# RWKV-7 / RG-LRU / cross-attention step: TensorE's order in the chunk chain fixed, and 48 projection steps ahead of the inverse instead of 37

## The chip, the cores and the metric

The kernel runs on one core of one Trainium2 chip. The metric is the device time of one launch in microseconds (us), the median of several runs. TensorE (PE in the profile, with its weight loads as PEld) multiplies; VectorE (DVE), ScalarE (ACT) and GpSimd (POOL) do the elementwise work; SyncE (SP) issues most DMAs. Each engine takes its instructions in a fixed order, and waits on semaphores for the others.

## The reference, cut to what matters

One layer for 512 prompt tokens and 8 samples of 8 tokens (N = 576 columns), width 1024. One projection feeds three branches; each is gated and projected, the three are merged, and an output projection and a norm follow:

```python
u, za, xb, zb, q, zc, gates = split_in(rmsnorm(x, g_norm) @ w_in)
oa, s_last, shift_last = rwkv7_branch(u, za, ...)   # 16 heads of 64
ob, h_last, conv_last = rglru_branch(xb, zb, ...)
oc = cross_attn(q, zc, mem_k, mem_v)
merged = g_a * (oa @ w_br_a) + g_b * (ob @ w_br_b) + g_c * (oc @ w_br_c)
y = rmsnorm(x + merged @ w_out, g_final)
```

The RWKV-7 branch is a recurrence over time with a 64x64 state per head:

```python
sa = einsum("bhvk,bhk->bhv", s, -kk_t)
s  = s * w_t + sa * (kk_t * a_t) + v_t * k_t      # outer products
o_t = einsum("bhvk,bhk->bhv", s, r_t)
```

## The kernel before, in words

**Projections as fill.** Each product of a 128-row block of weights with the 576 activations is a `Unit`. Weights and activations are each split into a high and a low part (`whi` by ACT at L280, `wlo` by DVE at L281; `xh`, `xl`), and three of the four products are summed. `Stream.step` issues one step: one of 8 slices of the inner dimension, 3 products on 2 halves of the columns, so 6 matmuls of 128x288 (L355). A unit is 8 steps. `st.go(n)` puts n steps into the program. Units come from two lists: `first` (what is needed next: the `u` units of the RWKV input, the `za` units of its gate) and, when that is empty, `fill` (`spill_units`, in this order: 24 gate units `g`, 8 `zc`, 8 `xb`, 8 `zb`), whose results are spilled to memory. A `zc` unit costs, besides its matmuls, one ACT pass and two DVE passes (L411, L415), a load of `ocd` and a store to `ocz`; a `g` unit has one ACT pass and a store.

**The RWKV branch** (`rwkv_phase`) takes the 16 heads as 8 pairs in 4 groups of 2 pairs, and time in 8 prompt chunks of 64 tokens; a ninth "chunk" holds the 64 sample tokens. For each group: prepare (`prep_a`, `prep_b`, `prep_c`); the products `m` (L990); `invert`, which sends 32x32 triangular blocks through memory to DVE, inverts them there in 60 small operations (`Xt`, `X`, L1016 and L1018), copies (`XT`, L1022) and sends them back (`M`, `xz`); meanwhile on PE `direct` (`R`, `Zt`), `bonus` (`bon`, L959 and L960) and `st.go(37)`. Then `invert2` joins the 32-blocks to 64-blocks (`z` L1041, `w` L1050, with ACT copies between), `solved` makes `U` and `W`, and `chain` goes through the 8 chunks: `A` = `ZR` times the state (L1128, whole 128x128 matmuls), DVE adds it to `UV` (`plus_state`, L1121), `go(2)`, the new state's part `dS` (L1137), the output `A<-UV,M` (`outs`, L1113), `go(4)`. The sample state goes along: `sample_a` (load `sn`, transposes `s0t`) in chunks 1 and 4, `sample_b` (`A8`, L1189) in 2 and 5, `sample_c` (`dSs`, L1202, transposes `s1t`, store) in 3 and 6.

**Two kinds of matmul.** Projections, `A` from the state and transposes use the whole array (128*128 in the profile's rows). `z`, `w`, `U`, `W`, `dS`, `outs`, `A8` and `dSs` give a `tile_position` and use 32 or 64 of its columns (32*32, 128*64, 128*32); they are called tiled here, and a tiled run is a stretch of PE's program that holds only such matmuls.

**The order.** A scheduler, which works from its own estimate of readiness, orders each engine's instructions when the kernel is built; what stands in the program is a proposal. So the steps of later units, of the next chunk's `go` and of the sample work end up between the matmuls of a chunk.

**After the groups:** `gn_a`, `gn_t`, `gn_b` normalise the output and multiply by the gate `za`, and store it (`oad`). Then the rest of the `zb` units; `load_split` loads the attention output (`oxl<-ocz`, on SP), splits it into `oh` (ACT, L592) and `ol` (DVE, L593) for the 8 branch units `br` of branch c; then those of branch a beside the RG-LRU (`lru_phase`), of branch b, and the output projection (`final`, `fo`).

Of the kernel before, what the change touches and what calls it, by code (L numbers as in the profile page):

```python
# [46 lines left out]
class Kern:  # L47
    def __init__(self, ctx, tc, ins, outs):
# [7 lines left out]
        self.dq = 0  # L56

# [4 lines left out]
    def transpose(self, out, in_, rows):  # L62

        self.nc.tensor.transpose(out, in_, self.ident[:rows, :rows])  # L64
# [240 lines left out]
class Stream:  # L305
# [24 lines left out]
    def step(self):  # L330
# [22 lines left out]
        for q, (a, b) in enumerate(((hi, xh), (hi, xl), (lo, xh))):  # L353
            for o, t0, m in parts:
                nc.tensor.matmul(self.ps[:, o:o + m], a[:, k, :], b[:, k, t0:t0 + m],  # L355
                                 start=(k == 0 and q == 0), stop=(k == KC - 1 and q == 2))
# [111 lines left out]
def lru_phase(K, o2, then):  # L468
# [4 lines left out]
    with tc.tile_pool(name="lruc", bufs=1, reuse_waits="tile") as lc, tc.tile_pool(name="lru", bufs=2, reuse_waits="tile") as lp:  # L473
# [31 lines left out]
        def gates(j):  # L505
# [5 lines left out]
            for q, bh in enumerate((K.bah, K.bxh)):  # L511
                g = lp.tile([P, N], F32, tag=f"g{q}", name=f"g{q}")
                for s in range(2):
                    pg = K.psb(f"pg{q}")[:, 0:HN]
                    cs = slice(HN * s, HN * s + HN)
                    nc.tensor.matmul(pg, wbd[q][:, j, :], xc[:, cs], start=True, stop=True)
# [143 lines left out]
def attention(K, xp, qs, qf, kv):  # L660
# [6 lines left out]
    def p_scores(h, n):  # L667
# [45 lines left out]
    def s_keys(g, b):  # L713
# [88 lines left out]
def rwkv_phase(K):  # L802
# [5 lines left out]
    with ExitStack() as es:  # L808
# [90 lines left out]
        def prep_a(o):  # L899
# [5 lines left out]
            for s in range(2):  # L905
                cs = slice(HN * s, HN * s + HN)
                for n, (dst, bias) in enumerate(((tw, K.w0h), (ta, K.a0h))):
                    pl = K.psb("lora")[:, 0:HN]
                    nc.tensor.matmul(pl, wlh[:, n, :], xw2[n][:, cs], start=True, stop=False)
                    nc.tensor.matmul(pl, wll[:, n, :], xw2[n][:, cs], start=False, stop=True)  # L910
# [15 lines left out]
        def prep_b(o):  # L926
# [25 lines left out]
        def bonus(o):  # L952
# [3 lines left out]
            for s in range(2):  # L956
                cs = slice(HN * s, HN * s + HN)
                pb = K.psb("bon")[:, 0:HN]
                nc.tensor.matmul(pb, K.bones, hi[:, cs], start=True, stop=False)  # L959
                nc.tensor.matmul(pb, K.bones, lo[:, cs], start=False, stop=True)  # L960
                nc.vector.tensor_mul(o.bon[:, cs], pb, o.v[:, cs])

        def prep_c(o):
# [71 lines left out]
        def invert2(prs):  # L1035
            for g0 in (0, 9):
                pzs = [K.psb("z1") for o in prs]
                for g in range(g0, g0 + 9):
                    for o, pz in zip(prs, pzs):
                        a, b = o.br, o.br + 32  # L1040
                        nc.tensor.matmul(pz[b:b + 32, 32 * (g - g0):32 * (g - g0) + 32], o.M1[a:a + 32, g, b:b + 32],  # L1041
# [5 lines left out]
                for g in range(g0, g0 + 9):  # L1047
                    for o, pw in zip(prs, pws):
                        a, b = o.br, o.br + 32
                        nc.tensor.matmul(pw[a:a + 32, 32 * (g - g0):32 * (g - g0) + 32], o.xz[b:b + 32, g, :],  # L1050
# [5 lines left out]
        def direct(prs):  # L1056

            r0 = prs[0].r0 = [rt.tile([P, N], F32, tag="k", name="r0") for _ in range(2)]
            for c0, n in ((0, 4), (4, 4), (8, 1)):
                pR = K.psb("R")  # L1060
                for c in range(c0, c0 + n):
                    for h in range(2):
                        for o in prs:
                            a, b, m = o.kr, o.br, P * (c - c0) + C * h
                            nc.tensor.matmul(pR[b:b + 64, m:m + C], o.M1[a:a + 64, 2 * c + h, b:b + 64],
# [7 lines left out]
            for c0 in (1, 5):  # L1073
                pZ = K.psb("Zt")
                for c in range(c0, c0 + 4):
                    for o in prs:
                        b, m = o.br, P * (c - c0)
                        nc.tensor.matmul(pZ[b:b + 64, m:m + P], o.ZR[:, c, 1 - o.q, :], K.ident, start=True, stop=True,
# [3 lines left out]
        def solved(prs):  # L1082

            r0, zt = prs[0].r0, prs[0].zt
            for c0, n in ((0, 4), (4, 4), (8, 1)):
                pU = K.psb("U")
                for c in range(c0, c0 + n):
                    for h in range(2):
                        for o in prs:
                            b, m = o.br, P * (c - c0) + C * h  # L1090
                            rhs = r0[c // 4][b:b + 64, m:m + C] if c < 8 else r0[h][b:b + 64, P * 4:N]
                            nc.tensor.matmul(pU[b:b + 64, m:m + C], o.M1[b:b + 64, 2 * c + h, b:b + 64],
# [15 lines left out]
        def outs(os, c, pA, first):  # L1108

            for h in range(2):  # L1110
                for o in os:
                    a, m = o.kr, P * o.q + C * h
                    nc.tensor.matmul(pA[a:a + 64, m:m + C], o.M1[:, 2 * c + h, a:a + 64], o.UV[:, c, C * h:C * h + C],  # L1113
                                     start=first, stop=(h == 1) or first, tile_position=(0, a), skip_group_check=True)
# [8 lines left out]
        def chain(os, c):  # L1123
            cur, nxt = sbd[(c + 1) % 2], sbd[c % 2]
            pA = K.psb("A")
            if c > 0:
                for o in os:
                    nc.tensor.matmul(pA[:, P * o.q:P * o.q + P], o.ZR[:, c].rearrange("p a b -> p (a b)"), cur[:, o.q, :],  # L1128
                                     start=o is os[0], stop=False, skip_group_check=True)
# [378 lines left out]
```

## Time and profile before

| what | value |
|---|---|
| median of 3 runs | 1184.54 us (1183.98 to 1185.02) |
| the profiled execution's own time | 1184.47 us |
| its span on the core | 1182.7 us |
| mean granted TensorE clock | 0.992 |
| PE / DVE / ACT / POOL busy | 1145.4 / 713.2 / 517.3 / 184.3 us |

The span is what the profile's instructions cover; 1.8 us of the execution lie around it. A group of rows counts matmuls as the chip runs them: an fp32 one is two of the program's where it uses the tiled form (`dS` x4 is `dS` x2 in the program). Busy time of pipelined matmuls overlaps, so a matmul's cost is read from the start of one to the start of the next.

### The profile page before, as it was taken

The page shows a single profiled execution, that of the slowest core. Times are in us where ns is not written, and L with a number is a line of the kernel's source. Part 1 is how long each engine was busy: PE and PEld are TensorE (multiplying, and loading weights), DVE is VectorE, ACT ScalarE, POOL GpSimd, SP SyncE. Part 2 cuts the span into 40 slices and gives each one's busy share as a digit, 9 for nine tenths or more (in the row PEclk, how much of TensorE's full clock was granted, in tenths as well). Part 3 has the DMA queues.
Part 4 walks back from the last instruction along what each step waited for, and adds up shares of the span by engine and source line. Part 5 has one row for each costly group of instructions (what it writes and reads, how often), then busy time and mean ns, then how long its engine had stood idle before and what let it go on. Part 6 is the DMA issues. An engine that isn't in the chain of part 4 may idle for free.

```text
span 1182.7 us, 25731 instructions
## 1 busy us (share of the span) xinstructions
PE 1145.4 (97%) x10567; PEld 1068.8 (90%) x10567; DVE 713.2 (60%) x1436; ACT 517.3 (44%) x1004; POOL 184.3 (16%) x311
## 2 busy tenths in 40 slices
PE   6999999999999999999999999999999999979997
PEld 4998877899998898988989989999889999979997
DVE  5345655238764687835788457874455386975633
ACT  5444544337324374243752336532444266442333
POOL 3010001010003210022100130101211012570031
PEclk9999999999999999999999999999999999998999
DMA  4447685522452233532233522345337665348412
GB/s 140 130 145 233 211 254 189 162 81 66 107 140 73 65 93 82 142 89 70 78 92 120 145 73 65 106 125 149 85 90 232 203 195 170 104 115 261 117 45 81
DMA packets 220623, 151.50 MB, mean 128 GB/s; under 512 B 52640, under 2 KB 196106, under 8 KB 220506
## 3 DMA queue, kind: packets, MB, share of 16 engines
q1 hardware_dynamic: 217242, 146.87, 42.1%
q10 hardware_dynamic: 3264, 2.99, 0.9%
q8 instruction: 83, 1.36, 0.5%
q14 instruction: 34, 0.28, 0.1%
HBM read 120.82 MB, written 29.01 MB: 127 GB/s over the span
## 4 chain that ended last, share of the span: by engine, by line
PE 79%; DVE 7%; ACT 5%; issue 3%; DMA 3%; POOL 2%; SPq 0%; DVEq 0%; ACTq 0%; POOLq 0%
PE u L355 13%; PE g L355 12%; PE br L355 9%; PE xb L355 4%; PE zc L355 4%; PE za L355 4%; PE fo L1349 4%; PE q L355 4%; PE zb L355 3%; PE kv L355 2%; PE m L990 1%; PE dS L1137 1%; DVE wlo L281 1%; DMA wraw<-in_w_mem_kv 1%; PE skt L64 1%
## 5 line engine op out<-in xcount | busy, mean ns | idle before, releaser
L280 ACT CAST whi<-wraw 128x1024 fp32r<-128x1024 f32 x129 | 135.4, 1050 | 292.6 <-PE g L355 90.7
L281 DVE TENSOR_TENSOR wlo<-wraw,whi 128x1024 fp32r<-128x1024 f32 x128 | 158.9, 1241 | 127.5 <-ACT whi L280 126.7
L355 PE MATMUL u<-xh,whi 128*128 128x288 f32 x400 | 92.2, 305 | 0.0
L355 PE MATMUL br<-oh,wlo 128*128 128x288 f32 x384 | 84.4, 302 | 4.4 <-DVE wlo L281 4.3
L355 PE MATMUL u<-xl,whi 128*128 128x288 f32 x400 | 88.6, 300 | 0.0
L355 PE MATMUL u<-xh,wlo 128*128 128x288 f32 x400 | 88.6, 299 | 0.0
L355 PE MATMUL br<-oh,whi 128*128 128x288 f32 x384 | 85.4, 305 | 3.0 <-ACT oh L592 2.9
L355 PE MATMUL g<-xh,whi 128*128 128x288 f32 x384 | 86.6, 304 | 0.0
L355 PE MATMUL g<-xh,wlo 128*128 128x288 f32 x384 | 84.7, 300 | 0.0
L355 PE MATMUL g<-xl,whi 128*128 128x288 f32 x384 | 84.4, 301 | 0.0
L355 PE MATMUL br<-ol,whi 128*128 128x288 f32 x384 | 84.2, 301 | 0.0
L355 PEld LDWEIGHTS u<-xh,whi 128*128 128x128 f32 x400 | 65.1, 188 | 5.5 <-issue 4.1
L355 PEld LDWEIGHTS br<-oh,wlo 128*128 128x128 f32 x384 | 63.5, 194 | 5.6 <-DVE wlo L281 5.6
L355 PEld LDWEIGHTS br<-oh,whi 128*128 128x128 f32 x384 | 63.7, 193 | 4.3 <-ACT oh L592 3.4
L355 PEld LDWEIGHTS u<-xl,whi 128*128 128x128 f32 x400 | 64.7, 188 | 2.0 <-issue 1.4
L355 PEld LDWEIGHTS u<-xh,wlo 128*128 128x128 f32 x400 | 64.7, 188 | 0.9 <-issue 0.2
L355 PEld LDWEIGHTS g<-xh,whi 128*128 128x128 f32 x384 | 62.3, 190 | 3.2 <-issue 3.1
L355 PEld LDWEIGHTS g<-xh,wlo 128*128 128x128 f32 x384 | 62.7, 190 | 1.2 <-issue 1.2
L355 PEld LDWEIGHTS br<-ol,whi 128*128 128x128 f32 x384 | 63.4, 193 | 0.1
L355 PEld LDWEIGHTS g<-xl,whi 128*128 128x128 f32 x384 | 62.4, 190 | 1.1 <-issue 1.1
L1016 DVE TENSOR_TENSOR Xt<-X 72x30 f32<-72x30 f32 (+14 forms) x120 | 39.3, 328 | 11.4 <-DMA X<-d 7.8
L1349 PE MATMUL fo<-wol,oh 128*128 128x256 f32 (+1 forms) x160 | 45.0, 282 | 0.0
(386 smaller groups left out, 2894.3 us busy)
## 6 DMA issues: line engine op xcount, KB each, us to landing
wraw<-in_w_in SPq DMA_DIRECT2D x89, 512.0 KB
wraw<-in_w_mem_kv SPq DMA_DIRECT2D x16, 512.0 KB
kn<-in_cache_mem_k SPq DMA_DIRECT2D x16, 512.0 KB
kn<-in_cache_mem_v SPq DMA_DIRECT2D x16, 512.0 KB
gd<-flt SPq DMA_DIRECT2D x24, 288.0 KB
gtt<-gd SPq DMA_DIRECT2D x24, 288.0 KB
wraw<-in_w_br_c SPq DMA_DIRECT2D x8, 512.0 KB
wraw<-in_w_br_a SPq DMA_DIRECT2D x8, 512.0 KB
```

Source lines behind the costliest of these rows:

```text
L64: self.nc.tensor.transpose(out, in_, self.ident[:rows, :rows])
L280: nc.scalar.copy(hi, raw)
L281: eng.tensor_sub(lo, raw, hi.bitcast(F32))
L355: nc.tensor.matmul(self.ps[:, o:o + m], a[:, k, :], b[:, k, t0:t0 + m], start=(k == 0 and q == 0), stop=(k == KC - 1 and q == 2))
L990: nc.tensor.matmul(pms[h][64 * w:64 * w + 64, P * (c - c0):P * (c - c0) + P], BK[64 * h:64 * h + 64, c, w, :], ZR[64 * h:64 * h + 64, c].r ...
L1016: nc.vector.tensor_mul(tv, X[:, 0:s, s:s + 1].to_broadcast([NQ, s, m]), X[:, s:s + 1, s + 1:].to_broadcast([NQ, s, m]))
L1137: nc.tensor.matmul(pS[hs, C * o.q:C * o.q + C], o.BKn[:, c, hs], o.UV[:, c, hs], start=True, stop=True, tile_position=(0, 64 * h))
L1349: nc.tensor.matmul(pos[t][:r, :W], a[:, k, t * P:t * P + r], b[:, k, :], start=(k == 0 and q == 0), stop=(k == KC - 1 and q == 2))
```

## The change

It adds a flag `K.pin` and a helper `K.mm`; while the flag is set (over the chain of a group) every matmul and transpose keeps its place in the program. The chain is rewritten so that a chunk has one stretch of whole matmuls (`A`, `full()`, 12 of fill) and one of tiled ones (`dS`, `outs`, `tiled()`), and then 24 of fill. The sample work is cut into five pieces, which are handed to chosen chunks; the load of `sn` is a piece of its own, ahead of the chain for the first pair and in chunk 3 for the second. And 48 steps stand ahead of the inverse's use instead of 37. The number of matmuls is the same. The core of the diff:

```diff
     def transpose(self, out, in_, rows):
-        self.nc.tensor.transpose(out, in_, self.ident[:rows, :rows])
+        ins = self.nc.tensor.transpose(out, in_, self.ident[:rows, :rows])
+        if self.pin:
+            self.tc.keep_in_program_order(ins)
+
+    def mm(self, *a, **kw):
+        ins = self.nc.tensor.matmul(*a, **kw)
+        if self.pin:
+            self.tc.keep_in_program_order(ins)
...
-        def chain(os, c):
+        def chain(os, c, full, tiled):
...
                 plus_state(os, c, pA)
+            full()
+            if c > 0:
                 st.go(2)
...
             outs(os, c, pA, c == 0)
             for o in os:
                 o.cur = nxt[:, o.q, :]
+            tiled()
             st.go(4)
...
-            st.go(37)
+            st.go(48)
...
+            fulls = {1: lambda: sample_a(o0), 4: lambda: sample_c(o0), 5: lambda: sample_a(o1)}
+            tileds = {2: lambda: sample_b(o0), 3: lambda: [sample_o(o0), sample_in(o1)],
+                      6: lambda: sample_b(o1), 7: lambda: sample_o(o1)}
+            sample_in(o0)
+            K.pin = True
             for c in range(8):
-                chain(prs, c)
-                if c in (1, 4):
-                    sample_a(prs[c // 4])
-                if c in (2, 5):
-                    sample_b(prs[c // 4])
-                if c in (3, 6):
-                    sample_c(prs[c // 4])
+                chain(prs, c, fulls.get(c, none), tileds.get(c, none))
+            K.pin = False
+            sample_c(o1)
```

`sample_o` holds the sample rows' `outs` and `dSs`, cut from `sample_b` and `sample_c`. In the changed kernel's rows every matmul has line L71 and every transpose L65, and other lines are up to 20 further down.

What this does to the order is seen at three places. **First, PE in chunk 1 of the first group's chain** (`u`, `g`: fill; `s0t`: a sample transpose). Before:

```order
L355 MATMUL u_4386<-xl,whi 128x288 x2
L355 MATMUL u_4386<-xh,wlo 128x288 x2
L1137 MATMUL dS<-UV,BKn 64x64 x2
L64 MATMUL s0t<-ident,sn 128x128
L1137 MATMUL dS<-UV,BKn 64x64 x2
L1113 MATMUL A<-UV,M_3281 64x64
L1113 MATMUL A<-UV,M_3428 64x64
```

Now:

```order
L71 MATMUL g_4038<-xh,whi 128x288 x2
L71 MATMUL g_4038<-xl,whi 128x288 x2
L71 MATMUL g_4038<-xh,wlo 128x288 x2
L71 MATMUL dS<-UV,BKn 64x64 x4
L71 MATMUL A<-UV,M_3281 64x64
L71 MATMUL A<-UV,M_3428 64x64
```

Before, the four `dS` stand in two tiled runs with a transpose between; now in one, and the fill beside them is of `g` units where it was of `u` units. Over the whole program the tiled runs go from 144 to 92. In the four chains, `U` and `W` with chunk 0 left out, they go from 64 (17, 17, 15 and 15) to 28 (7 each); in `invert2`, `solved` and chunk 0 from 5 a group to 1.

**Second, DVE in the inverse of group 2** (`flt`: results of fill units; `zc_7900`: one such unit in PSUM). Before:

```order
L1018 TENSOR_TENSOR X<-X,Xt 72x9x22
L1016 TENSOR_TENSOR Xt<-X 72x210
L1018 TENSOR_TENSOR X<-X,Xt 72x10x21
L1016 TENSOR_TENSOR Xt<-X 72x220
L1018 TENSOR_TENSOR X<-X,Xt 72x11x20
```

Now:

```order
L1027 TENSOR_TENSOR X<-X,Xt 72x9x22
L290 TENSOR_TENSOR wlo<-wraw,whi 128x1024
L1025 TENSOR_TENSOR Xt<-X 72x210
L420 SCALAR_TENSOR_TENSOR flt<-flt,zc_7900 128x576
L1027 TENSOR_TENSOR X<-X,Xt 72x10x21
L424 SCALAR_TENSOR_TENSOR flt<-flt 128x576
L1025 TENSOR_TENSOR Xt<-X 72x220
```

The 60 operations of the inverse are the same. Between the first of them and `XT` stand 4 `wlo`, 1 `wls` and 4 `flt` operations before, and 5, 1 and 10 now; in groups 0 and 1 the count is unchanged, and in group 3 there are 4 `wlo` and no `flt` operation now, where there were 4 and 4.

**Third, PE and SP behind the last chain.** PE before, at the end of the last `za` unit:

```order
L355 MATMUL za_10853<-xl,whi 128x288 x2
L355 MATMUL za_10853<-xh,wlo 128x288 x2
L64 MATMUL ro<-ident,shst 125x128
L64 MATMUL ro<-ident,shst 100x128
L355 MATMUL zb_10971<-xh,whi 128x288 x2
L355 MATMUL zb_10971<-xl,whi 128x288 x2
```

PE now:

```order
L71 MATMUL za_11207<-xl,whi 128x288 x2
L71 MATMUL za_11207<-xh,wlo 128x288 x2
L65 MATMUL ro<-ident,shst 125x128
L65 MATMUL ro<-ident,shst 100x128
L71 MATMUL br_11354<-oh,whi 128x288 x2
L71 MATMUL br_11412<-oh,whi 128x288
L71 MATMUL br_11354<-ol,whi 128x288 x2
```

SP now, from the first pair's `oad` on:

```order
L61 DMA oad<-oT 128x576
L61 DMA out_shift_p<-rowbuf 25x128
L61 DMA out_shift_s<-rowbuf 100x128 x2
L61 DMA wraw<-in_w_br_c 128x8x128
L61 DMA oad<-oT 128x576
L61 DMA oxl<-ocz 128x576 x8
```

Between the last `za` matmul and the first `br` matmul PE had six `zb` units (288 matmuls); now it has two transposes, since the fill lists have run out. On SP the eight `oxl` loads stand behind the second `oad`, as they did before (there in two parts, of 5 and 3).

More of the change, by code (lines that the diff above doesn't have):

```diff
@@ L515, in gates @@
                     cs = slice(HN * s, HN * s + HN)
-                    nc.tensor.matmul(pg, wbd[q][:, j, :], xc[:, cs], start=True, stop=True)
+                    K.mm(pg, wbd[q][:, j, :], xc[:, cs], start=True, stop=True)
                     nc.scalar.activation(g[:, cs], pg, AF.Tanh, bias=bh[:, j:j + 1], scale=0.5)
@@ L931, in prep_b @@
             for c in range(NCH):
-                nc.tensor.matmul(pr_[br:br + 64, 2 * c:2 * c + 2], o.sq[:, C * c:C * c + C], K.bones2, start=True, stop=True,
+                K.mm(pr_[br:br + 64, 2 * c:2 * c + 2], o.sq[:, C * c:C * c + C], K.bones2, start=True, stop=True,
                                  tile_position=(0, br))
@@ L958, in bonus @@
                 pb = K.psb("bon")[:, 0:HN]
-                nc.tensor.matmul(pb, K.bones, hi[:, cs], start=True, stop=False)
-                nc.tensor.matmul(pb, K.bones, lo[:, cs], start=False, stop=True)
+                K.mm(pb, K.bones, hi[:, cs], start=True, stop=False)
+                K.mm(pb, K.bones, lo[:, cs], start=False, stop=True)
                 nc.vector.tensor_mul(o.bon[:, cs], pb, o.v[:, cs])
@@ L1077, in direct @@
                         b, m = o.br, P * (c - c0)
-                        nc.tensor.matmul(pZ[b:b + 64, m:m + P], o.ZR[:, c, 1 - o.q, :], K.ident, start=True, stop=True,
+                        K.mm(pZ[b:b + 64, m:m + P], o.ZR[:, c, 1 - o.q, :], K.ident, start=True, stop=True,
                                          tile_position=(0, b))
@@ L1112, in outs @@
                     a, m = o.kr, P * o.q + C * h
-                    nc.tensor.matmul(pA[a:a + 64, m:m + C], o.M1[:, 2 * c + h, a:a + 64], o.UV[:, c, C * h:C * h + C],
-                                     start=first, stop=(h == 1) or first, tile_position=(0, a), skip_group_check=True)
+                    K.mm(pA[a:a + 64, m:m + C], o.M1[:, 2 * c + h, a:a + 64], o.UV[:, c, C * h:C * h + C],
+                         start=first, stop=(h == 1) or first, tile_position=(0, a), skip_group_check=True)
             for o in os:
@@ L1136, in chain @@
                     hs = slice(C * h, C * h + C)
-                    nc.tensor.matmul(pS[hs, C * o.q:C * o.q + C], o.BKn[:, c, hs], o.UV[:, c, hs], start=True, stop=True,
-                                     tile_position=(0, 64 * h))
+                    K.mm(pS[hs, C * o.q:C * o.q + C], o.BKn[:, c, hs], o.UV[:, c, hs], start=True, stop=True,
+                         tile_position=(0, 64 * h))
             pS3 = pS[:, 0:G * C].rearrange("p (q v) -> p q v", v=C)
@@ L1168, in sample_a @@
                     nc.sync.dma_start(sn[64 * b2:64 * b2 + 64, :, 64 * h:64 * h + 64], src[b2])
+        def sample_a(o):
+            sn = o.sn
             pt = K.psb("s0t")
@@ L1201, in sample_c @@
                 hs = slice(C * h, C * h + C)
-                nc.tensor.matmul(pS[hs].rearrange("p (b v) -> p b v", v=C), o.BKn[:, 8, hs], o.uvx[:, :, hs],
-                                 start=True, stop=True, tile_position=(0, 64 * h))
+                K.mm(pS[hs].rearrange("p (b v) -> p b v", v=C), o.BKn[:, 8, hs], o.uvx[:, :, hs],
+                     start=True, stop=True, tile_position=(0, 64 * h))
             nc.vector.tensor_add(s1, s1, pS.rearrange("p (b v) -> p b v", v=C))
+        def sample_c(o):
+            s1 = o.s1
             so = big("so")[:, 0:4, :]
```

49 lines of the change are left out of this document (26 added, 23 removed).

## Prediction

> **What bounds the kernel now.** I read the page first, then the windows of the stages that the change touches, then timelines of single places. From the page:
>
> ```profile
> span 1182.7 us, 25731 instructions
> PE 1145.4 (97%) x10567; PEld 1068.8 (90%) x10567; DVE 713.2 (60%) x1436; ACT 517.3 (44%) x1004; POOL 184.3 (16%) x311
> PE   6999999999999999999999999999999999979997
> PEclk9999999999999999999999999999999999998999
> ```
>
> PE is busy nearly everywhere; the one slice below 9 between the ends is the 37th. So time can be won only by making PE's own work denser, and is lost wherever PE has to wait. The windows of the inverse in group 2, of the `zb` units behind the last chain, and of the RG-LRU's end (PE busy, PEld, DVE, ACT, POOL, granted clock, DMA share, GB/s):
>
> ```profile
> 621.00:663.00 42.00, 42.00 (x329) 41.80 (x328) 33.95 (x81) 10.77 (x16) 3.80 (x4) 1.00 0.47 135
> 897.00:936.00 39.00, 39.00 (x295) 39.00 (x295) 18.17 (x21) 15.54 (x23) 0.06 (x2) 1.00 0.74 242
> 1035.00:1065.00 30.00, 22.99 (x151) 21.48 (x151) 24.05 (x25) 12.46 (x18) 23.51 (x24) 0.93 0.41 115
> ```
>
> In the first two PE has no idle time: the fill covers a wait of other engines. In the third it idles 7.0 of 30 us. The amount of fill is fixed, so the change can only move this cover: 11 steps in each of 4 groups. A step is 6 matmuls; `zb` below takes 38.40 us for 288, 0.133 us each, so a step is 0.80 us, 48 steps are 38.4 us, and 44 steps moved are 35.2 us.
>
> **Part 1, fewer tiled runs: a gain.** Two chunks' ends in group 0's chain, PE's timeline; in the first `dS` is split, in the second whole:
>
> ```profile
> 373.29 0.34 PE L1137 MATMUL dS<-UV,BKn 128*64 128x64 f32 x4
> 373.56 0.40 PE L355 MATMUL u<-xh,whi 128*128 128x288 f32 x1
> 373.88 0.34 PE L1137 MATMUL dS<-UV,BKn 128*64 128x64 f32 x4
> 374.05 0.40 PE L1113 MATMUL A<-UV,M 128*64 128x64 f32 x8
> 374.38 0.40 PE L355 MATMUL u<-xh,whi 128*128 128x288 f32 x1
> ...
> 378.93 0.45 PE L1137 MATMUL dS<-UV,BKn 128*64 128x64 f32 x8
> 379.21 0.41 PE L1113 MATMUL A<-UV,M 128*64 128x64 f32 x8
> 379.55 0.53 PE L355 MATMUL u<-xh,whi 128*128 128x288 f32 x2
> ```
>
> Split, the same eight `dS` and eight `A` matmuls go from 373.29 to 374.38, 1.09 us with one `u` of 0.133 inside; whole, 0.62 us. A run more therefore costs 1.09 - 0.62 - 0.13 = 0.34 us. The four chains lose 36 runs: 12.2 us at least. Some runs were also entered late:
>
> ```profile
> 402.62 0.34 PE L1137 MATMUL dS<-UV,BKn 128*64 128x64 f32 x4 [0.24 <-DVE UV L1121]
> ```
>
> 0.24 us of waiting stand ahead of this one. If every second run lost such a wait too, a run would be worth 0.34 + 0.12 = 0.46 us, and 36 of them 16.6 us. I take 16, near the upper end, since single-operation runs (`dSs`, `A8`) also disappear into longer ones: **-16 us (-12.2 to -16.6)**.
>
> By the Trainium skill, "TensorEngine Tiling (Array Packing)", Tiling Modes, a change of the tiling mode, not only of the tile, drains TensorE; a run that goes from 64 columns (`dS`) to 32 (`A8`) would then drain inside as well. By that rule the 8 runs with `A8` would keep the price of one run each, 8 x 0.34 = 2.7 us, and the gain would be 13.
>
> **Part 2, `invert2`, `solved` and chunk 0 in one run: nothing.** Four runs fewer a group, 1.4 us, but before a fill unit stood between `z`, its ACT copy and `w`; now PE waits for the copies:
>
> ```profile
> 349.36 0.39 ACT L1045 COPY xz<-z 32x288 f32<-32x288 f32 x1 [0.17 <-PE z L1041]
> ```
>
> Two pairs make 0.78 us of copies per pass, and two passes some 1.4 us of waiting, so gain and wait cancel: **0 (-2 to +2)** for the four groups.
>
> **Part 3, the chain's order: a small loss.** `dS` needs `UV` from DVE, and 12 matmuls (1.6 us) now stand between `A` and `dS`, no more and no less.
>
> ```profile
> 377.73 0.61 PE L1128 MATMUL A<-sbd,ZR 128*128 128x128 f32 x4
> 378.38 0.61 DVE L1121 TENSOR_TENSOR UV<-A,UV 64x128 f32<-64x128 f32 x2 [1.32 <-PE A L1128]
> ```
>
> From the start of `A` to the end of the two adds it is 1.26 us here, which fits; where a `wlo` and an `flt` operation (rows below, 1.2 and 0.75) are ahead of the adds in DVE's queue, it is late by up to 1.6 us. I take one or two chunks a group with about 0.2: **+1 (0 to +4)**. The new `sn` loads go on SP ahead of the chain, where nothing waits for them.
>
> **Part 4, group 2's inverse is late: a loss.** DVE's groups inside the inverse of group 2, its first and last operation, PE's first fill and first `z`, and, from group 0, SP's issue of the second pair's blocks:
>
> ```profile
> L281 DVE TENSOR_TENSOR wlo<-wraw,whi 128x1024 fp32r<-128x1024 f32 x4 | 4.9, 1218 | 0.8 <-ACT whi L280 0.8
> L415 DVE SCALAR_TENSOR_TENSOR flt<-flt 128x576 f32<-128x576 f32 x2 | 1.5, 754 | 1.3 <-DMA flt<-ocd 1.3
> L411 DVE SCALAR_TENSOR_TENSOR flt<-flt,zc 128x576 f32<-128x576 f32 x2 | 1.5, 745 | 0.0
> ...
> 624.25 0.19 DVE L1016 TENSOR_TENSOR Xt<-X 72x30 f32<-72x30 f32 x1 [1.42 <-DMA X<-d]
> 654.73 1.10 DVE L1022 COPY XT<-X 36x1024 f32<-36x1024 f32 x1
> ...
> 621.55 0.43 PE L355 MATMUL g<-xh,whi 128*128 128x288 f32 x2
> 661.90 0.75 PE L1041 MATMUL z<-xz,M 32*32 32x32 f32 x18
> ...
> 346.36 1.04 SPq L1032 DMA_DIRECT2D M<-d  x2
> ```
>
> The inverse starts 2.7 us after the fill, runs 31.6 us to 655.83, and `z` of the first pair starts 6.1 us later. Now DVE has one `wlo` (1.22) and six `flt` operations (0.75 each) more in between, 5.7 us, since the fill there is six `zc` units: it ends at 2.7 + 31.6 + 5.7 = 40.0 us, `z` is ready at 46.1, and about 1.0 later (the issue of its blocks) for the second pair, whose matmuls now stand in the same run: 47.1. The fill ends at 38.4. **PE waits 8.5 us.** At least 6.4, if DVE's idle time in the rows (0.8 and 1.3) takes up new work; at most 11.1, if two more `ocd` loads make DVE wait 1.3. In groups 0 and 1 nothing is added on DVE:
>
> ```profile
> 311.41 0.43 PE L355 MATMUL g<-xh,whi 128*128 128x288 f32 x2
> 348.57 0.75 PE L1041 MATMUL z<-xz,M 32*32 32x32 f32 x18
> ```
>
> 37.2 us from fill to `z`, and some 38.2 for the second pair, against 38.4: just covered. In group 3 DVE's `flt` operations are gone, so it is earlier than before.
>
> **Part 5, behind the last chain: a loss.** The chain of waits, then SP, ACT and DVE there:
>
> ```profile
> 897.26 0.22 PE ro L64 x2
> 897.47 38.40 PE zb L355 x288
> ```
>
> ```profile
> 900.89 0.35 SPq L60 DMA_DIRECT2D oad<-oT x1
> 901.29 3.44 SPq L60 DMA_DIRECT2D oxl<-ocz x5
> 907.54 3.01 SPq L60 DMA_DIRECT2D oxl<-ocz x3
> 905.86 2.16 ACT L592 CAST oh<-oxl 128x576 fp32r<-128x576 f32 x3 [0.62 <-DMA oxl<-ocz]
> 916.38 0.76 DVE L593 TENSOR_TENSOR ol<-oxl,oh 128x576 fp32r<-128x576 f32 x1 [0.21 <-ACT oh L592]
> ```
>
> From the end of `za` (897.26) to the last `ol` (917.14) pass 19.9 us: the second `oad` must be issued first (4 us), the first load lands 4.6 us later, and eight loads take 10. The `zb` units hid all of it. Now PE has two transposes and, before the last `ol`, some 47 matmuls of the first two `br` units, 0.2 + 6.3 us. The eight loads now go out together, which at best saves the 2.8 us between 904.73 and 907.54; I take half: 18.5 - 6.5 = **+12 us (9.5 to 15)**. What is late next is the RG-LRU, whose work stands beside `br` as before; the 7.0 us of idle in its window stay, or shrink a little.
>
> **Part 6, the clock behind a long wait.** PE's timeline at a wait of 2.97 us, and a window behind it:
>
> ```profile
> 1065.40 0.85 PE L355 MATMUL br<-oh,wlo 128*128 128x288 f32 x2 [2.97 <-DVE wlo L281]
> 1066.05 0.68 PE L355 MATMUL br<-oh,whi 128*128 128x288 f32 x2
> 1069.41 0.68 PE L355 MATMUL br<-ol,whi 128*128 128x288 f32 x2
> ...
> 1066.00:1068.00 2.00, 2.00 (x11) 2.00 (x10) 2.00 (x4) 0.18 (x2) 0.57 (x1) 0.50 0.96 305
> ```
>
> From 1066.05 to 1069.41 two matmuls take 0.48 us instead of 0.27, and the granted clock is 0.50. In the 4.5 us from 1065.40 to 1069.89 the 19 matmuls would need 2.5: 2.0 us lost. Parts 4 and 5 make one long wait each. Behind `z` I take the 2.0, behind `za` 0.5, since there loads set the pace: **+2.5 (0 to 4)**.
>
> By the Trainium skill, "TensorE: Matmul & The Clock Gate", Part 1, a window of about 3.4 us without work halves the clock, and about 3.4 us of work restore it; by that figure each long wait would cost an estimated 1.7 us. The rows agree, except that a recorded idle time of 2.97 us was enough.
>
> **The sum.** -16 + 0 + 1 + 8.5 + 12 + 2.5 = +8.0 us. The profiled execution took 1184.47 us, its span and 1.8 us around it, the median 1184.54; so 1184.5 + 8 = **1192.5 us**.
>
> **The rivals.**
> - *Forecast, the two waits outweigh the runs*: 1188 to 1199. For it: the rows of parts 4 and 5 and both orders.
> - *The wait behind `za` does not come*, at one place: the `oxl` loads. If they leave SP while `za` still runs and land under it, part 5 and its clock go: 1192.5 - 12 - 0.5 = 1180, faster. It decides if that wait stays under some 2 us (12.5 less the 8.0 + 2.4 that separate the forecast from faster). For it: `ocz` is complete long before. Against it: `oad` stands ahead in SP's queue and needs the gate of `za`. If group 2's wait also stays away, 1180 - 8.5 - 2 = 1169.5.
> - *They cancel*: both waits come at half their size, or the RG-LRU's 7.0 idle us shrink by most: 1192.5 - 7 to 10, 1182 to 1186.
> - *The pinned order makes PE wait in the chain*: nothing may slip between `A` and `dS` any more. At 0.5 us in each of 28 chunks it is 14 us, not 1: 1205. Against it: the 1.26 us above, and DVE busy only 60% of the span.
> - *The change does not do what it says*: if a run's price lies in the `dS` and `A` matmuls themselves and goes with them, the gain is perhaps a third, 5 us: 1203. Against it: the two chunk ends quoted.
>
> **How the numbers follow.** Forecast 0.51; the `za` wait absent 0.18 and both late waits absent 0.08 (faster, 0.26); cancelling 0.12; waits in the chain 0.06 and no price of runs 0.05 (slower with the forecast, 0.62). 0.2%, 2.4 us, is about what can be told from no change. The range goes from 1179, which takes in the faster rival's 1180, to 1203: the upper ends of parts 4 and 5 and the lower end of part 1 give 1192.5 + 2.6 + 3 + 3.8 = 1201.9, and I leave 1 for part 3. Left out are 1169.5 and 1205. The forecast's own range is 1188 to 1199.
>
> **What would show it.** Right: tiled stretches of `dS` and `A` at about 0.62 us with no split; PE idle some 8 us ahead of `z` in group 2, none in 0, 1 and 3; idle some 12 us ahead of and in the first `br` unit, with the releaser ACT `oh` or DVE `ol`; the granted clock at 0.5 behind both. Wrong: `oxl` issued ahead of the end of `za`; the inverse of group 2 as long as before; waits for `UV` ahead of most `dS`; chain stretches no shorter than before.

## The result, and the profile after

The changed kernel takes 1188.83 us (median of 6 runs), the kernel before 1184.78 beside it: ratio 1.0052, 95% interval 1.0037 to 1.0067. By that ratio it is slower by 6.2 us (the two medians lie 4.1 apart); 8.0 had been forecast. The profiled execution took 1189.0 us. The page:

```profile
span 1187.3 us, 25700 instructions
PE 1135.4 (96%) x10567; PEld 1071.7 (90%) x10567; DVE 713.0 (60%) x1436; ACT 514.4 (43%) x1004; POOL 187.4 (16%) x311
PE   6999999999999999999999899999999699989997
PEclk9999999999999999999999979999999799989999
```

PE's busy time fell by 10 us although its matmuls are the same; the table below shows where. But there are two new dents in PE's row, and the granted clock has a dent with each or in the slice behind it.

To place the difference I counted the time between fixed points of PE's program, less 0.1333 us for each projection matmul (128x288) in between, which leaves what is not fill. In us, from the starts in PE's timeline, summed over the four groups where a row has four parts:

| stretch | before | after | difference | forecast |
|---|---|---|---|---|
| wait ahead of the first `z` | 0.4 | 6.1 | +5.7 (group 2 alone) | +8.5 |
| first `z` to first `dS` | 35.4 | 42.2 | +6.8 | 0, and 2 for the clock |
| first `dS` to `ot` (the chain) | 89.1 | 71.2 | -17.8 | -16 + 1 |
| `ot` to the first `br` | 1.3 | 11.9 | +10.7 | +12 |
| first `br` to the first `fo` | 29.5 | 31.3 | +1.8 | 0.5 for the clock |

With small rests these make +7.5 us from group 0's first `m` to the end. From PE's first matmul to that point the changed kernel's profiled execution was 2.6 us faster (99.7 against 102.2); there nothing differs in what was changed, and in all profiled executions this stretch lies anywhere between 99.5 and 104.1.

**The chain.** PE's timeline at chunk 1 of group 0; `dS` whole:

```profile
363.79 0.42 PE L71 MATMUL g<-xh,wlo 128*128 128x288 f32 x2
364.14 0.45 PE L71 MATMUL dS<-UV,BKn 128*64 128x64 f32 x8
364.42 0.40 PE L71 MATMUL A<-UV,M 128*64 128x64 f32 x8
364.75 0.54 PE L71 MATMUL g<-xh,whi 128*128 128x288 f32 x2
...
370.20 0.45 PE L71 MATMUL dS<-UV,BKn 128*64 128x64 f32 x8
370.48 0.40 PE L71 MATMUL A<-UV,M 128*64 128x64 f32 x8
370.81 1.08 PE L71 MATMUL A<-sbs,zx 128*32 128x128 f32 x32
371.82 0.54 PE L71 MATMUL g<-xh,whi 128*128 128x288 f32 x2
```

From `dS` to the next `g` it is 0.61 us, nearly the same at each chunk end of this kind, and no wait for `UV` stands ahead of any `dS` of a chunk with fill around it.

**Group 2's inverse.** DVE's groups between its first operation and `XT`, its first and last operation, and PE's first fill and first `z`:

```profile
L290 DVE TENSOR_TENSOR wlo<-wraw,whi 128x1024 fp32r<-128x1024 f32 x5 | 6.1, 1216 | 0.8 <-ACT whi L289 0.8
L424 DVE SCALAR_TENSOR_TENSOR flt<-flt 128x576 f32<-128x576 f32 x5 | 3.8, 753 | 0.2 <-DMA flt<-ocd 0.2
L420 DVE SCALAR_TENSOR_TENSOR flt<-flt,zc 128x576 f32<-128x576 f32 x5 | 3.7, 744 | 0.0
...
642.86 0.19 DVE L1025 TENSOR_TENSOR Xt<-X 72x30 f32<-72x30 f32 x1 [2.26 <-DMA X<-d]
676.63 1.14 DVE L1031 COPY XT<-X 36x1024 f32<-36x1024 f32 x1
...
639.32 0.43 PE L71 MATMUL zc<-xh,whi 128*128 128x288 f32 x2
683.50 2.30 PE L71 MATMUL z<-xz,M 32*32 32x32 f32 x33 [5.63 <-DMA xz<-d]
```

The inverse starts 3.5 us after the fill (before 2.7) and takes 34.9 us (before 31.6), `z` starts 44.2 us after the fill (38.4 of which is fill), and the clock behind it is near half. Windows of the inverse, of `z` to `dS` in group 2, of group 1 from within the last `w` pass to 4 us past the first `dS`, of the wait ahead of `br`, and of the first `br` matmuls:

```profile
638.00:680.00 42.00, 39.88 (x300) 39.49 (x296) 36.10 (x85) 10.87 (x15) 3.83 (x4) 1.00 0.59 173
683.00:696.00 13.00, 11.90 (x282) 11.50 (x284) 1.56 (x3) 4.44 (x11) 0.37 (x3) 0.53 0.44 106
517.00:527.00 10.00, 9.77 (x210) 9.50 (x208) 2.65 (x6) 3.21 (x9) 2.00 (x3) 0.83 0.40 115
927.00:938.00 11.00, 0.96 (x8) 0.71 (x6) 3.05 (x4) 2.16 (x5) 2.64 (x10) 0.67 0.78 237
938.00:944.00 6.00, 5.52 (x22) 5.47 (x23) 4.50 (x6) 4.06 (x7) 0.00 (x0) 0.50 1.00 320
```

**`z` to `dS`.** The third of these was not expected: in group 1 PE's one recorded wait from `z` to `dS` was 0.47 us, and the clock fell all the same. PE in group 0, with the same wait, and ACT's copy that it waits for:

```profile
346.95 1.22 PE L71 MATMUL z<-xz,M 32*32 32x32 f32 x36
350.35 1.86 PE L71 MATMUL w<-M,xz 32*32 32x32 f32 x35 [0.47 <-ACT xz L1054]
352.20 3.79 PE L71 MATMUL U<-r,M 64*64 64x64 f32 x66
...
349.91 0.80 ACT L1054 COPY xz<-z 32x288 f32<-32x288 f32 x2
```

The 66 `U` matmuls take 3.79 us here; the same in the kernel before took 2.14, at full clock:

```profile
359.17 2.14 PE L1092 MATMUL U<-r,M 64*64 64x64 f32 x66
...
348.60:362.80 14.20, 14.08 (x324) 13.04 (x323) 2.79 (x4) 5.68 (x13) 0.00 (x0) 1.00 0.45 134
```

**Behind the last chain.** PE, SP, ACT and DVE:

```profile
927.58 0.38 PE L65 MATMUL ro<-ident,shst 128*125 128x128 f32 x2
938.48 1.09 PE L71 MATMUL br<-oh,whi 128*128 128x288 f32 x3 [10.52 <-ACT oh L601]
...
931.36 0.36 SPq L61 DMA_DIRECT2D oad<-oT  x1
931.77 9.76 SPq L61 DMA_DIRECT2D oxl<-ocz  x8
...
937.76 0.67 ACT L601 CAST oh<-oxl 128x576 fp32r<-128x576 f32 x1 [8.33 <-DMA oxl<-ocz]
```

As forecast: `oad` first, then the loads, then the casts, and nothing for PE to do. But the eight loads, side by side in SP's order, did not go out together: they left over 9.8 us, and each of the last three 0.03 us after an `ol` had freed one of the five buffers that the kernel gives `oxl`. From the end of `za` to the last `ol` it is 18.3 us.

### The profile page after: what moved, and what is told of

It reads as the page before. It is cut to its first block, busy times and chain, and to the rows that moved or that the text cites. A ratio compares the mean times of both kernels' runs of the same rounds, so it can differ in the third digit from the quotient of the medians.

```text
span 1187.3 us, 25700 instructions
## 1 busy us (share of the span) xinstructions
PE 1135.4 (96%) x10567; PEld 1071.7 (90%) x10567; DVE 713.0 (60%) x1436; ACT 514.4 (43%) x1004; POOL 187.4 (16%) x311
## 3 DMA queue, kind: packets, MB, share of 16 engines
q1 hardware_dynamic: 217242, 146.87, 42.2%
## 4 chain that ended last, share of the span: by engine, by line
PE 77%; DVE 10%; ACT 5%; DMA 4%; issue 3%; POOL 1%; SPq 0%; DVEq 0%; ACTq 0%
PE u L71 14%; PE g L71 11%; PE br L71 10%; PE xb L71 4%; PE zb L71 4%; PE fo L71 4%; PE q L71 4%; PE za L71 3%; PE A L71 2%; PE kv L71 2%; PE zc L71 2%; PE m L71 1%; PE U L71 1%; PE dS L71 1%; DMA wraw<-in_w_mem_kv 1%
## 5 line engine op out<-in xcount | busy, mean ns | idle before, releaser
L71 PE MATMUL br<-oh,whi 128*128 128x288 f32 x384 | 86.6, 309 | 13.5 <-ACT oh L601 13.4
L71 PE MATMUL u<-xh,whi 128*128 128x288 f32 x400 | 88.7, 303 | 0.0
L71 PE MATMUL br<-oh,wlo 128*128 128x288 f32 x384 | 85.0, 304 | 3.7 <-DVE wlo L290 3.6
L71 PE MATMUL g<-xh,whi 128*128 128x288 f32 x384 | 86.2, 303 | 0.0
L71 PE MATMUL u<-xl,whi 128*128 128x288 f32 x400 | 85.7, 295 | 0.0
L71 PE MATMUL u<-xh,wlo 128*128 128x288 f32 x400 | 85.6, 295 | 0.0
L71 PE MATMUL br<-ol,whi 128*128 128x288 f32 x384 | 85.1, 304 | 0.0
L71 PE MATMUL g<-xh,wlo 128*128 128x288 f32 x384 | 83.8, 298 | 0.0
L71 PE MATMUL g<-xl,whi 128*128 128x288 f32 x384 | 83.3, 298 | 0.0
L71 PEld LDWEIGHTS br<-oh,whi 128*128 128x128 f32 x384 | 64.6, 196 | 14.9 <-ACT oh L601 14.2
L71 PEld LDWEIGHTS u<-xh,whi 128*128 128x128 f32 x400 | 63.8, 188 | 5.9 <-issue 5.5
L71 PEld LDWEIGHTS br<-oh,wlo 128*128 128x128 f32 x384 | 64.1, 196 | 5.2 <-DVE wlo L290 5.2
L71 PEld LDWEIGHTS g<-xh,whi 128*128 128x128 f32 x384 | 61.7, 188 | 3.5 <-issue 3.1
L71 PEld LDWEIGHTS u<-xh,wlo 128*128 128x128 f32 x400 | 64.5, 188 | 0.0
L71 PEld LDWEIGHTS u<-xl,whi 128*128 128x128 f32 x400 | 64.5, 188 | 0.0
L71 PEld LDWEIGHTS br<-ol,whi 128*128 128x128 f32 x384 | 64.2, 196 | 0.1
L71 PEld LDWEIGHTS g<-xh,wlo 128*128 128x128 f32 x384 | 62.0, 188 | 0.9 <-issue 0.9
L71 PEld LDWEIGHTS g<-xl,whi 128*128 128x128 f32 x384 | 61.9, 188 | 0.8 <-issue 0.8
L1130 DVE TENSOR_TENSOR UV<-A,UV 64x128 f32<-64x128 f32 x64 | 18.5, 289 | 53.4 <-PE A L71 52.2
```

The lines of the kernel that those rows point to most:

```text
L71: ins = self.nc.tensor.matmul(*a, **kw)
L1130: nc.vector.tensor_add(u, pA[o.br:o.br + 64, P * o.q:P * o.q + P], u)
```

## The experiments

The theory: the tiled runs gain about 17 us; the 11 steps that moved ahead of the inverse are needed there, but the fill that they take away uncovers the loads behind the last chain, and the `zc` units that now stand in group 2's inverse make DVE late. A rival for each was tried. Ratios are to the kernel before, from five rounds each. The stretches of the table above, in us:

| kernel | ratio (95%) | ahead of `z` | `z` to `dS` | chain | to `br` | to `fo` |
|---|---|---|---|---|---|---|
| changed | 1.0052 (1.0037 to 1.0067) | 6.1 | 42.2 | 71.2 | 11.9 | 31.3 |
| e1_pin_37 | 1.0219 (1.0205 to 1.0233) | 30.5 | 48.2 | 73.9 | 1.2 | 30.2 |
| e2_48_only | 1.0059 (1.0045 to 1.0073) | 0.4 | 37.6 | 84.1 | 11.6 | 31.8 |
| e3_fill_order | 0.9983 (0.9974 to 0.9992) | 0.4 | 40.3 | 71.3 | 11.7 | 31.5 |
| e4_za_early | 1.0034 (1.0022 to 1.0046) | 5.6 | 42.0 | 71.3 | 8.2 | 33.4 |
| e5_fill_za | 0.9967 (0.9954 to 0.9980) | 0.4 | 40.1 | 71.4 | 7.2 | 33.1 |
| e6_fill_in_zw | 0.9895 (0.9881 to 0.9910) | 0.4 | 29.0 | 71.0 | 12.9 | 29.3 |
| e8_z_then_w | 0.9907 (0.9894 to 0.9920) | 0.4 | 27.7 | 71.4 | 11.6 | 32.2 |
| e11_oad_pool | 0.9969 (0.9956 to 0.9981) | 0.4 | 40.3 | 71.4 | 6.9 | 32.9 |
| e15_last_go2 | 1.0006 (0.9989 to 1.0023) | 5.8 | 41.7 | 71.2 | 4.1 | 32.1 |
| e13_zw_last_go2 | 0.9865 (0.9844 to 0.9885) | 0.4 | 27.9 | 71.2 | 4.0 | 33.5 |
| e12_zw_za_go2 | 0.9867 (0.9845 to 0.9890) | 0.4 | 28.9 | 71.3 | 6.3 | 30.5 |
| e14_fill_za_go2 | 0.9901 (0.9882 to 0.9921) | 0.4 | 28.6 | 71.4 | 10.0 | 32.7 |

**The two parts apart: e1_pin_37 and e2_48_only.** The first is the changed kernel, the second the kernel before, each with one number:

```diff
-            st.go(48)
+            st.go(37)
```

> The changed kernel with 37 steps ahead of the inverse's use again, and the order pinned as it is. Theory: the gain of the tiled runs (17.8 us in the two traces) stays, and the zb units are back behind the last chain, so the 10.8 us wait there goes; but now the inverse is not covered: its data is ready about 38 us after the fill begins, 37 steps end at 29.6, so PE waits about 8 us in groups 0, 1 and 3 and about 13 in group 2, with about 2 us of lower clock behind each. Before -17.8 + 4.4 (z, w, U) + 37 + 8: about 1216 us, 1.026 times before. Rival (the 11 more steps are not needed once the order is fixed, and only the wait behind za hurts): 1172 us, 0.99 times before.

```diff
-            st.go(37)
+            st.go(48)
```

> The kernel before with 48 steps for 37 and nothing else: the scheduler still orders the chains, and puts 9 us more fill between the steps and z in group 2. Theory: tiled runs cost what they cost before, the inverse is covered everywhere, and only the wait behind za comes (no zb units are left there): before + 12 to 13 us, 1197 us, ratio 1.0105. Rival (the wait behind za is an effect of the pinned order, or is made good in the RG-LRU's stage): within 3 us of before.

e1_pin_37: 1.0219, the theory's side, a little less than its 1.026. The first `z` of group 0:

```profile
347.31 0.90 PE L71 MATMUL z<-xz,M 32*32 32x32 f32 x13 [6.03 <-DMA xz<-d]
```

PE waited 6.2, 5.9, 9.7 and 8.7 us ahead of `z`, and the wait ahead of `br` is gone. So with the order fixed, the steps ahead of the inverse are needed: nothing else goes between. The chains gain 15.1 us here, of the changed kernel's 17.8.

e2_48_only: the wait ahead of `br` is there without any pinned order. Its lines, and the window of `z` to `dS` in group 0:

```profile
930.15 0.38 PE L64 MATMUL ro<-ident,shst 128*125 128x128 f32 x2
940.70 0.61 PE L355 MATMUL br<-oh,whi 128*128 128x288 f32 x1 [10.16 <-ACT oh L592]
...
346.99:361.22 14.23, 14.00 (x312) 13.00 (x311) 1.97 (x4) 4.64 (x12) 0.00 (x0) 0.88 0.42 115
```

It comes from the steps alone, 10.3 us. Two more losses were not expected: `z` to `dS` costs 2.2 us more than before, with the clock at 0.88 and 0.89 in groups 0 and 2 though PE has no recorded wait there, and the stretch to `fo` 2.3 more. The ratio, 1.0059, is still less than the 1.0105 expected, since the chain costs 5.0 us less than before. That is not the number of tiled runs (65 in the chains, 64 before): 1.5 us are recorded waits that are gone, and where the rest comes from was not found. In group 2 the inverse is as slow as in the changed kernel (33.9 us), but here fill stands ahead of `z` until 7.7 us after `XT`; so the wait in the changed kernel needed the fixed order as well. That the profiled stretches make 10 us and the timed runs 7 is left open; the first stretch of the program, which varies by 4.6 us, can hide such a difference in single profiles.

**Group 2's inverse: e3_fill_order.**

```diff
     us += [Unit(w, C_ZB + P * j, ...) for j in range(KC)]
+    g, zc = us[0:24], us[24:32]
+    us[12:16], us[22:24], us[24:26], us[26:32] = zc[0:4], zc[4:6], zc[6:8], g[12:16] + g[22:24]
     return us
```

> The changed kernel with the list of fill units in another order: the 8 zc units, which have two DVE operations each, go to the chains and the preparation of groups 0 to 2, and six g units, with none, stand in group 2's inverse. The same work. Theory: PE's 5.6 us wait ahead of z in group 2 and the lower clock behind it (12.4 us from z to dS there against 9.5 in groups 1 and 3) go: 8 us less than the changed kernel, ratio to before 0.998 to 0.999. Rival (group 2 waits for the transfers, not for DVE): no difference from the changed kernel, 1.005.

0.9983, within the theory's range. PE's fill and `z` in group 2, now with no wait, and DVE's first and last operation of the inverse, which takes 27.5 us:

```profile
677.83 0.42 PE L71 MATMUL xb<-xh,wlo 128*128 128x288 f32 x2
678.19 1.22 PE L71 MATMUL z<-xz,M 32*32 32x32 f32 x36
...
643.88 0.19 DVE L1027 TENSOR_TENSOR Xt<-X 72x30 f32<-72x30 f32 x1 [2.89 <-DMA X<-d]
670.20 1.14 DVE L1033 COPY XT<-X 36x1024 f32<-36x1024 f32 x1
```

Against the changed kernel 0.0069 is won, 8 us: 5.7 ahead of `z` and 2.9 between `z` and `dS` of group 2 (12.4 to 9.5), while group 3 gives 1.2 back there (9.5 to 10.7). DVE's work was the cause: the `zc` units' loads moved away with it, but DVE had waited only 0.2 us for them in the changed kernel's rows above. One permutation of a list makes the whole change a small gain.

**The place behind the last chain: e4_za_early, e5_fill_za, e11_oad_pool.** e4 is the changed kernel with

```diff
+            if g + 1 == NG:
+                st.add(*[za_unit(o.p) for o in prs])
             sample_in(o0)
             K.pin = True
...
-            st.add(*[za_unit(o.p) for o in prs])
+            if g + 1 < NG:
+                st.add(*[za_unit(o.p) for o in prs])
```

> The changed kernel with the last group's two za units ahead of its chain in the list, so that they run in the chain in place of zb units, and two zb units stand behind the chain. The same work. Theory: the loads of the attention output wait on SP for the second oad, which waits for za; oad now follows the transposes ot at once, about 5 us earlier, and the wait of 10.8 us behind za shrinks by 4 to 6: ratio to before 1.000 to 1.002. Rival (the loads themselves, or the transfers ahead of them, set the time): no difference, 1.005.

e5 is e3 and e4 together, and e11 adds to it

```diff
-            K.dma(K.oad[o.p], oT)
+            nc.gpsimd.dma_start(K.oad[o.p], oT)
```

and the same queue for the two shift outputs.

> The two edits of e3_fill_order and e4_za_early together, otherwise the changed kernel. Theory: they act at two places (z of group 2, the start of br), so they add: 0.9983 - 0.0018, ratio 0.9965 to before. Rival (one wait moves into the other, or into the RG-LRU's stage): 0.998, no better than the order of the fill alone.

> e5_fill_za with the stores of oad and of the shift rows on POOL's DMA queue, so that on SP nothing which needs the last group's output stands ahead of the oxl loads. The same work. Theory: the loads wait for their place in SP's queue, not for data or memory; they leave about 6 us earlier and PE's wait of 6.9 us ahead of br goes, with the lower clock behind it: 6 to 8 us less than e5_fill_za, ratio to before 0.990 to 0.9915. Rival (the transfers' own 10 us, or the loads waiting for memory that the last group holds): under 2 us less.

e4_za_early won 3.7 us of the wait but gave 2.2 back behind it: 1.0034, between theory and rival. e5_fill_za: the edits add (0.9967). e11_oad_pool: the rival. The first loads and casts of e11, with the window in which the loads are on their way, then those of e5_fill_za:

```profile
919.60 2.60 SPq L61 DMA_DIRECT2D oxl<-ocz  x5
926.96 2.97 ACT L603 CAST oh<-oxl 128x576 fp32r<-128x576 f32 x5 [3.27 <-DMA oxl<-ocz]
920.00:925.00 5.00, 2.33 (x18) 2.09 (x16) 4.09 (x4) 1.60 (x2) 4.47 (x7) 1.00 1.02 286
...
923.52 2.49 SPq L61 DMA_DIRECT2D oxl<-ocz  x5
926.89 0.67 ACT L603 CAST oh<-oxl 128x576 fp32r<-128x576 f32 x1 [3.54 <-DMA oxl<-ocz]
```

The loads left SP ahead of `oad` and 3.9 us earlier than in e5_fill_za, but the first cast, which waited for its load in both, began at the same time: 7.4 us after the first issue in e11, 3.4 in e5. The DMA engines are full while the loads of e11 are on their way (share 1.02), and its five casts then run with no further wait, so the five loads had landed close together. An earlier place in the queue wins nothing here; that the full engines are the reason is argued from the share, and no run tried them with less to do.

**The joined run of `z`, `w`, `U`, `W`: e6_fill_in_zw, e8_z_then_w.** Both start from e3_fill_order and pin `invert2` as well. e6 puts a step behind each of the four passes and takes them from behind chunk 7:

```diff
                 for o, pz in zip(prs, pzs):
                     nc.scalar.copy(o.xz[...], pz[...])
+                st.go(1)
...
             tiled()
-            st.go(4)
+            if c < 7:
+                st.go(4)
```

> e3_fill_order with one step of fill (6 whole matmuls) behind each of the four z and w passes of a group, pinned, and the four steps taken from behind chunk 7. The same work. In the changed kernel the granted clock falls to 0.68 to 0.83 in the joined run of z, w, U and W, though no wait there is over 0.7 us; before it was 1.00. Theory: z and w alone (32x32 tiles, waits for ACT) are too little work for the clock, so whole matmuls between them keep it at 1.00, and the time from z to dS without fill falls from 10.7, 9.3, 9.5 and 10.7 us to about 8.8: 5 us less than e3_fill_order, ratio to before 0.994. Rival (only the waits for the ACT copies count, and the clock falls through U and W): clock still under 0.9, at most 2 us less, 0.9966 or more.

e8 puts no fill in, but closes the loop over the two halves behind the copies of `z` and opens it again for `w`:

```diff
                     nc.scalar.copy(o.xz[...], pz[...])
+            for g0 in (0, 9):
                 pws = [K.psb("w12") for o in prs]
```

> e3_fill_order with both z passes ahead of both w passes, pinned, so that PE no longer waits for a copy between them more than once; no fill in between. The same work. Theory (small matmuls without whole ones lower the clock): the run is some 0.5 us shorter per group, and the granted clock in it still falls below 0.9: ratio to before 0.996 to 0.998. Rival (the waits lower the clock): clock 1.00 and z to dS about 8.5 us, 5 us less than e3_fill_order, 0.994.

The windows of `z` to `dS` in group 0, of e3_fill_order and then of e6 and e8:

```profile
348.00:359.00 11.00, 10.52 (x286) 10.04 (x286) 2.24 (x4) 4.50 (x12) 0.00 (x0) 0.69 0.59 176
```

```profile
347.00:357.50 10.50, 10.38 (x309) 9.34 (x308) 2.15 (x5) 4.55 (x12) 0.00 (x0) 1.00 0.62 184
```

```profile
348.60:356.00 7.40, 7.15 (x296) 6.62 (x296) 2.43 (x5) 4.88 (x12) 0.00 (x0) 1.00 0.49 138
```

Both held the clock at 1.00 and won more than expected: from `z` to `dS` 29.0 and 27.7 us for the four groups, against 40.3 and, in the kernel before, 35.4. My theory, that the 32x32 matmuls themselves are too little work, does not hold: e8 has as many of them in a row. Where the wait of 0.47 us for the copy is gone, so is the fall of the clock, in all four groups of both (one group of e12, below, is an exception whose cause stays open). The pin of `invert2`, which both also have, was not tried by itself. PE waits once there now:

```profile
350.25 1.58 PE L71 MATMUL w<-M,xz 32*32 32x32 f32 x70 [0.17 <-ACT xz L1056]
```

Of the 11 to 13 us won, the clock is the larger part by an estimate: the recorded wait is 0.47 us a group in e3_fill_order and 0.17 in e8, 1.2 us for the four groups, while the some 20 us at half clock (worked out in the last section) cost up to 10. The two were not measured apart. e8 needs no fill and keeps the four steps.

**More fill for the end: e15, e13, e12, e14.** e15 is the changed kernel, e13 e8_z_then_w, with

```diff
-            st.go(4)
+            st.go(4 if os[0].p < 2 * (NG - 1) else 2)
```

at the end of `chain`; e12 is e13 with e4's edit, e14 e6_fill_in_zw with both (there `go(2)` for c < 7).

> The changed kernel with 2 instead of 4 steps behind each chunk of the last group's chain only, so that 16 steps (12.8 us) of fill are left for behind it. The same work. Theory: those steps cover nothing in the chain, so there is no new wait there; behind the chain they stand partly ahead of za, which delays oad by some 3 us, and a zb unit stands behind za: the wait ahead of br falls from 10.8 to about 6, ratio to before about 1.001. Rival (the chain needs four steps a chunk): waits for UV or the state of 0.5 us and more in most chunks, no gain.

> e8_z_then_w with the same two steps a chunk in the last group. Theory as in e15_last_go2: 0.9907 - 0.004 to 0.005, ratio 0.986. Rival (gains in different places don't add, since the RG-LRU's stage has its own chain): 0.990.

> e13_zw_last_go2 with the last group's za units ahead of its chain as in e4_za_early, so that all of the fill that is left, 25 us, stands behind the chain while oad follows ot at once. Theory: the loads of the attention output, about 14 us from the first issue to the last ol, now lie under zb; the wait ahead of br falls below 2 us and the clock stays at 1.00 there: 12 us less than e8_z_then_w, ratio 0.980 to 0.982. Rival (the transfer engines, which are full there, are slower still with zb's stores and weights beside the loads): a wait of 5 us stays, 0.985.

> The same two edits (za early, two steps a chunk in the last group) on e6_fill_in_zw. Theory: as in e12_zw_za_go2, 12 us less than e6_fill_in_zw, ratio 0.979 to 0.982, the clock at 1.00 from the first group to br. Rival: as there, 0.984.

e15 and e13 as expected: the wait ahead of `br` falls from 11.9 and 11.6 to 4.1 and 4.0 us, and the last chain, with half the fill behind its chunks, costs nothing more (16.2 us against 16.3). e12 and e14 missed: the fill covers the loads, and a new wait takes their place. PE and ACT in e12:

```profile
918.10 0.85 PE L71 MATMUL br<-oh,whi 128*128 128x288 f32 x2 [4.64 <-ACT whi L289]
...
917.01 1.03 ACT L289 CAST whi<-wraw 128x1024 fp32r<-128x1024 f32 x1
```

The `whi` cast for the first `br` weights stands behind all eight `oh` casts in ACT's queue, so PE again starts only when the last load is in; a `whi` ahead of them was not tried. In e14 the same wait is 8.4 us. The rival's 0.985 lies in e12's interval, but what ended PE's wait is a cast that stands behind those of the loads, which the rival did not have. In e12 the clock also fell once in a `z` to `dS` stretch of e8's order, in group 3 (8.2 us instead of 6.9):

```profile
837.76:845.93 8.17, 7.71 (x281) 7.28 (x280) 2.64 (x5) 4.67 (x12) 0.00 (x0) 0.79 0.43 123
```

The best, e13 and e12, are alike: 0.9865 (0.9844 to 0.9885) and 0.9867.

## Why the prediction was right, step by step

- **Part 1, the tiled runs.** Right in sign and place: with part 3 the chains cost 17.8 us less, forecast 15. A run that is joined lasts 0.61 us at such a chunk end. But the 16 was made up otherwise: some 4 us of it were waits, and the recorded waits inside the chains fell by 1.8 (from 1.8 to none). The other 16.0 us make 0.45 us for each of the 36 runs, not 0.34; and e2, whose chains gain 3.5 us beside the waits with as many runs as before, shows that not all of it need be the runs. `A8` alone, in the kernel before, took 1.01 us from start to start,

```profile
389.78 1.08 PE L1189 MATMUL A<-sbs,zx 128*32 128x128 f32 x32
390.79 0.38 PE L1128 MATMUL A<-sbd,ZR 128*128 128x128 f32 x1
```

  and 1.01 inside the joined run (370.81 to 371.82). The step from `A` to it there is as long as the one from `A` to whole `g` matmuls (0.33 us; 370.48 to 370.81, and 364.42 to 364.75), so only the entry was saved. That agrees with the Trainium skill's "TensorEngine Tiling (Array Packing)", Tiling Modes, by which a change of mode drains TensorE. The whole gain was all the same more than my own 15, and not the 12 that the rule would have given (its 13 less part 3).
- **Part 2, `z` to `dS` in one run.** This is the term that was mis-sized: 0 (-2 to +2) forecast, +3.5 us measured in groups 0, 1 and 3 (26.3 to 29.8). The waits for the copies were seen, and were less than forecast (0.47 us recorded a group, 1.4 forecast), but the clock was put at nothing here: it fell to 0.68 in group 0. With the clock at 1.00, in e8, the stretch is 6.9 us a group against 8.7 before, so joining the runs gained even here, and the clock took more than that.
- **Part 3, waits for `UV`.** Forecast +1 (0 to 4); there is none in the fill-covered chunks. It is inside the 17.8.
- **Part 4, group 2's inverse.** Right in place, cause and neighbours (no wait in groups 0, 1 and 3); the size was 5.7, not 8.5, and under the range of 6.4 to 11.1 (by its own terms, 47.1 less 38.4, the wait would be 8.7). The inverse started 0.8 us later, but grew by 3.3 us, not 5.7: DVE's idle time in it fell by 1.3 us, and the rest is overlap of neighbouring operations in the record. `z` came 5.7 us after `XT`, not 6.1, with no extra 1.0 for the second pair; the 6.1 was read where fill stood ahead of `z`, and where PE waits in all groups, in e1, it is 4.7 to 5.2. e3 confirmed the cause.
- **Part 5, behind the last chain.** Right: 10.7 of 12, and 18.3 us to the last `ol`, forecast 18.5. The saving from loads that go out together did not come that way, as the last three waited for buffers. e2 showed that the steps cause the wait, and e11 that SP's order is not all of the reason: loads that left 3.9 us earlier, with the DMA engines at a share of 1.02, came no earlier.
- **Part 6, the clock.** Behind `z` of group 2 the long wait cost 2.9 us more than in e3 (12.4 to 9.5), where the clock was 0.82 and not 1.00; the stretch from `br` to `fo` is 1.8 us longer, not divided further; forecast 2.0 and 0.5. The first `br` matmuls ran at half clock (0.50 in the window above).
- **The rivals.** The loads did not leave early; the order did not make PE wait in the chain; the waits did not cancel the gain. That a too short run of steps is worse still (e1, +2.2%) had not been priced.
- **The sum.** That it came within 2 us is in part luck: the chains and group 2's wait were 2.8 us below their forecast each, `z` to `dS` in the other groups 3.5 above it, and the part behind `br` 1.3 above.

So the change is two trades. Fixing the order, with the steps, gains 17.8 us in the chains (15.1 without the steps), loses some of it to the clock in the joined run, and obliges the kernel to have 48 steps ready; those steps are worth their place there, but their absence at the end and the sort of unit that lands in group 2 cost the rest of the gain and more.

## What to carry to other kernels

When fill is moved, ask two questions of the place it leaves and the place it goes to: what did it hide there, and which other engines' work comes with it. Where a run of small matmuls waits for copies, order the passes so that each copy has another pass beside it; waits of half a microsecond can come with a lower clock for several. Read the clock in every stage that a change touches, not only where PE is idle for long.

## What the runs showed of the hardware that was not expected

- One recorded wait of 0.47 us among 32x32 matmuls (0.67 from start to start) went with a fall of the granted clock to half. The window, in e3_fill_order's group 0, where the wait ends at 351.53:

```profile
352.00:358.00 6.00, 6.00 (x140) 5.94 (x139) 1.10 (x2) 2.10 (x5) 0.00 (x0) 0.50 0.78 233
```

  From `z` to `dS` the clock was 0.68, 0.82, 0.82 and 0.68 in that kernel's four groups (10.7, 9.3, 9.5 and 10.7 us), which makes an estimated 6.8 us at half clock in groups 0 and 3 and 3.4 in the other two. It was under 1.00 in every group of the seven kernels that have this wait. Without it it was 1.00 in all groups of the kernel before, e6, e8, e13 and e14, but not everywhere: group 3 of e12_zw_za_go2, with e8's order, had 0.79, and groups 0 and 2 of e2_48_only 0.88 and 0.89. So the wait is not the only way to such a fall. By the Trainium skill, "TensorE: Matmul & The Clock Gate", Part 1, it takes a window of about 3.4 us without work; here PE was busy for most of every such stretch (10.52 of 11.00 us in the row of e3_fill_order above), so the measurement decides, and it says that less is enough. What share of idle time decides was not tried.
- With the DMA engines at a share of 1.02, the cast of the first of five loads could begin 7.4 us after the issue (e11), where it was 3.4 in e5_fill_za and 4.6 in the kernel before.
- The stretch ahead of group 0, the same work in all kernels, took from 99.5 to 104.1 us beside its fill in the profiled executions, more than the effect of some edits; differences under 5 us are read from stretches or from many runs, not from two spans.
